# The merge-gate columns of a hybrid decoder trunk: from plain three-term matmuls to a seven-product Strassen form, with h parked in DRAM

## The chip, the cores and the metric

The kernel runs on one core of one Trainium2 chip, in one launch. The metric is the device time of one execution in microseconds (us); the kernel before takes 928.23 us (median of three runs, 928.15 to 928.38).

## The reference, cut to what matters

One layer of a decoder trunk with 1024 tokens and 1024 channels:

```
h = rms_norm(x, g_pre)
s5_x, s5_g, lru_x, lru_g, gate_s, gate_l = split(h @ w_in)   # 512, 512, 1280, 1280, 1024, 1024 columns
y_s = S5 branch of s5_x (complex diagonal state space), GELU, GLU, times silu(s5_g), @ w_bs
y_l = causal conv and RG-LRU of lru_x, times silu(lru_g), @ w_bl
merged = sigmoid(gate_s) * y_s + sigmoid(gate_l) * y_l
x = x + rms_norm(merged @ w_out, g_post)
x = x + (p @ w_ple) * sigmoid(x @ w_ple_gate)
```

The change concerns the last 2048 columns of `w_in`, those of `gate_s` and `gate_l`. In blocks of 128 columns they are the column blocks 28 to 35 and 36 to 43.

## The kernel before

Everything is laid out with channels on the partitions and tokens along the free axis. A matrix product is cut in blocks of 128 x 128 of the weight against 128 x 512 of the data (one half of the tokens). For accuracy each float32 operand is split in a rounded part and the rest (`hi`, `lo`), and one block product is three matmuls, in `three`: hi by hi, hi by lo of the data, lo of the weight by hi.

Weights come from DRAM in chunks of up to eight blocks into `wraw` (four buffers), and are split, four blocks (one *quad*) at a time, into a ring `wq` of six buffers. `weight_plan` lists the quads in order of use; `Weights.ahead`, called before each use, makes the quad four places ahead. `make` copies the quad with ScalarE to `hi`. The `lo` is a subtraction on VectorE (`lows`); for the late matrices named in `BY_DMA` it is made otherwise: ScalarE writes the negated hi, and a DMA of GpSimd's queue adds the raw weight onto it. Some matrices further on (w_bl, w_out) already are in a Strassen form, with sums of weights that `sum` makes on GpSimd.

`h` stands in four quarters, `hq["B11"]`, `"B12"`, `"B21"`, `"B22"` (half of the channels, half of the tokens), each with a hi and a lo page of 1 MB.

The instruction order on TensorE, VectorE, ScalarE and GpSimd is the order in which the code is written; only SyncE's DMAs are ordered by a scheduler. Work beside the matmuls is written as generators in a list `bg`, and `tick()` advances each by one step; the loops of matmuls call it at fixed places, so a step of the side work has its fixed place between two groups of matmuls on every engine. All engines work through their orders without overtaking.

The stage that is changed I call the *light stage*. In it `light(m, ...)` makes one column block: `rows` runs 48 matmuls (eight blocks of channels, two halves of tokens, three terms) with a tick after each 12, ScalarE takes the sigmoid, SyncE stores it (`sgl_d`, `sgs_d`). Eighteen columns come this way: 36 to 43, 28 to 35, and 4 and 5 (these with silu). The side work of this stage is the S5 branch, `s5_all`: eight blocks `hb` in `s5_main`, each a chain over all engines: TensorE `pkt` and `pin`, ScalarE `kt` and `pq`, VectorE `ta`, `tb`, four scans, `q`; eight small DMAs that spread `kt` into `toep`; GpSimd's `s5_out_weights` for the next block (it reuses the buffer of `kt`, tile `t`, and so waits until those DMAs have landed); then TensorE `py` from `toep` and `q`. After the light stage comes the LRU stage (`lru_head`), where the same ring of weights goes on.

Of the kernel before, what the change touches and what calls it, by code (L numbers as in the profile page):

```python
# [13 lines left out]
ALU = mybir.AluOpType  # L14
# [18 lines left out]

F_ROWS = (0, 1, 4, 2, 5, 3, 6, 7)


def weight_plan():
    blocks, quads = [], []

# [9 lines left out]
    def col(name, m, ks):  # L49
        return [(name, k, m) for k in ks]  # L50
# [21 lines left out]

    for m in range(NL):
        gated(8 + m, m - 1)
        plain(col("w_in", 18 + m, range(ND)))
# [32 lines left out]
    for h in range(2):  # L108
# [3 lines left out]
        for c in cs[0 if h else 2:]:  # L112
            cut(c)
    return blocks, quads


BLOCKS, QUADS = weight_plan()

# [17 lines left out]
class Weights:  # L136
# [42 lines left out]
    def sum(self, upto):  # L179
        G = self.nc.gpsimd  # L180
        while len(self.ready) <= min(upto, len(QUADS) - 1):
            i = len(self.ready)
            self.fetch(i)
            q = QUADS[i]
            s = self.sums
            if q[0] == "O2" and len(self.done) < i:
# [20 lines left out]
            if q[0] in ("S4", "O4"):  # L207
                add("S4", "A12", "S2", ALU.subtract, "S2")
            if q[0] == "S3":
# [3 lines left out]
    def make(self, upto):  # L213
        nc = self.nc
        while len(self.done) <= min(upto, len(QUADS) - 1):
# [7 lines left out]
            q = QUADS[i]  # L223
            if q[0] == "plain" and BLOCKS[q[1][0]][0] in self.BY_DMA and i < len(QUADS) - 2 * ND:
                nc.scalar.activation(lo, src, AF.Copy, scale=-1.0)  # L225
                nc.gpsimd.dma_start(lo.bitcast(F32), src, accum_op=ALU.add)  # L226
            else:
                self.owed.append((i, lo, src, hi))
# [24 lines left out]
def tile_hybrid_trunk(  # L253
# [19 lines left out]
    pages = ctx.enter_context(tc.tile_pool(name="pages", bufs=1))  # L273
    page_pool = {i: pages for i in range(14)}

# [9 lines left out]
    y_d = dram.tile([NS, 8, 8, 16, P], F32, name="y_d")  # L285
    pt_d = dram.tile([2, 8, 32 * P], F32, name="pt_d")

    def cst(shape, name, value=None, dt=F32):
# [617 lines left out]
    def s5_main(hb, table, before):  # L906
# [20 lines left out]
        for g in range(4):  # L927
            T.matmul(ps[32 * g:32 * g + 16, :P], bb_1[:, 4 * hb + g, :],
                     ca[:, g, 0:8, :].rearrange("p d c -> p (d c)"), start=True, stop=True, tile_position=(0, 32 * g))
        for g in range(4):  # L930
            S.activation(kt[:, g, :], ps[32 * g:32 * g + 16, :P], AF.Copy)
        V.tensor_tensor(kt[:, :, 0:16], kt[:, :, 0:16], dd, ALU.add)
        for j in range(8):
            nc.sync.dma_start(toep[j::8, :, 16 * j:P], kt[:, :, 0:P - 16 * j])
        yield

        pin = px.tile([P, 2, 2, P], F32, tag="px", name=f"pin{hb}")
        for g in range(4):
            T.matmul(pin[:, g // 2, g % 2, :], win[:, g, :], U[:, g, :], start=True, stop=True)
        next(table, None)  # L940
# [86 lines left out]
    def u_last():  # L1027
# [3 lines left out]
        yield  # L1031

    bg.append(u_last())
    bg.append(s5_all())
    for m in range(ND):
        light(36 + m, sgl_d[m], False, ev_tile)
    for m in range(ND):
        light(28 + m, sgs_d[m], False, ev_tile)
    for m in range(2):
        light(4 + m, sil_d[m], True, ev_tile)  # L1040
    drain()
    s5x.close()
# [85 lines left out]
    for m in range(NL):  # L1128
        conv, early, gate, gates = lru_head(m)
        conv(rows(hplain, f"rx{m}", between=between))  # L1130
        bg.append(early())
        gate(rows(hplain, f"rg{m}"))
        between = gates
# [564 lines left out]
```

## Time and profile before

| what | us |
|---|---|
| runs | 928.15, 928.23, 928.38 |
| profiled execution, own time | 928.25 |
| its span on the core | 926.5 |
| TensorE busy with matmuls | 919.0 |
| VectorE, ScalarE, GpSimd busy | 624.6, 469.1, 150.6 |
| light stage (first `ps_L` to first `ps_rx` matmul) | 78.0 to 300.6 |

PE is TensorE's matmuls, PEld its weight loads, DVE VectorE, ACT ScalarE, POOL GpSimd, SP SyncE's DMA queue. The profiled execution's own time is 1.75 us more than its span, and it stands at the median of the runs. A row of the trace names a line of the code, an engine, the tile written and read, and a duration; a matmul's own duration (0.39 us) overlaps its neighbours', so what a matmul costs is read from the distance of two starts.

### The profile page before, as it was taken

How to read it: one execution, taken by the hardware profiler on the slowest of the kernel's cores; microseconds unless marked ns; L12 is line 12 of the kernel's file. 1: busy time of each engine (PE TensorE's matmuls, PEld its weight loads, DVE VectorE, ACT ScalarE, POOL GpSimd, SP SyncE). 2: the span in 40 equal slices, each digit the busy share in tenths (PEclk: the TensorE clock that was granted, in tenths of full speed). 3: DMA queues.
4: the chain of work that ended last, by engine and by line, in shares of the span. 5: the costliest groups of instructions: out<-in, count | busy, mean ns of one | idle time of the engine just before them, and what ended most of it. 6: DMA issues, size and time to landing. Idle time of an engine off the chain costs nothing.

```text
span 926.5 us, 11716 instructions
## 1 busy us (share of the span) xinstructions
PE 919.0 (99%) x4228; PEld 760.3 (82%) x4228; DVE 624.6 (67%) x977; ACT 469.1 (51%) x714; POOL 150.6 (16%) x159
## 2 busy tenths in 40 slices
PE   9999999999999999999999999999999999999997
PEld 7888888888888888888888888888888887887886
DVE  6885566666664347766666767687862798886863
ACT  6643233444443356666666668544534355558531
POOL 1218112212220000000000000022322126422100
PEclk9999999999999999999999999999999999999999
DMA  9745445564533201111111116811479975499951
GB/s 358 277 126 160 126 142 166 172 171 133 173 97 113 74 29 52 52 46 51 52 52 52 47 34 216 291 56 55 141 255 244 247 193 206 119 245 233 301 184 56
DMA packets 70442, 134.21 MB, mean 145 GB/s; under 512 B 18416, under 2 KB 32880, under 8 KB 70384
## 3 DMA queue, kind: packets, MB, share of 16 engines
q1 hardware_dynamic: 64768, 122.72, 41.7%
q0 software_dynamic: 5472, 10.49, 6.3%
q8 instruction: 33, 0.54, 0.2%
q10 hardware_dynamic: 144, 0.26, 0.1%
q14 instruction: 25, 0.20, 0.1%
HBM read 95.30 MB, written 27.53 MB: 133 GB/s over the span
## 4 chain that ended last, share of the span: by engine, by line
PE 89%; issue 6%; DMA 2%; DVE 1%; POOL 1%; ACT 0%; POOLq 0%; SPq 0%
PE ps_L L319 16%; PE ps_L L317 8%; PE ps_rx L319 8%; PE ps_rg L319 8%; PE ps_rg L317 4%; PE ps_rx L317 4%; PE ps_F L319 3%; PE ps_u L319 3%; PE bZ L319 3%; PE ps_pg L319 2%; PE bW L319 2%; PE pg L319 2%; PE bX L319 2%; PE ps_ple L319 2%; PE ps_ea L319 2%
## 5 line engine op out<-in xcount | busy, mean ns | idle before, releaser
L319 PE MATMUL ps_L<-hB,wq 128*128 128x512 f32 x640 | 197.4, 390 | 0.0
L319 PEld LDWEIGHTS ps_L<-hB,wq 128*128 128x128 f32 x640 | 120.3, 188 | 24.3
L317 PE MATMUL ps_L<-hB,wq 128*128 128x512 f32 x320 | 127.1, 397 | 0.0
L222 ACT ACTIVATE wq<-wraw 128x512 fp32r<-128x512 f32 (+1 forms) x188 | 112.5, 613 | 24.1 <-issue 9.2
L234 DVE TENSOR_TENSOR wq<-wraw,wq 128x512 fp32r<-128x512 f32 (+1 forms) x152 | 105.0, 706 | 3.1 <-ACT wq L222 3.1
L319 PE MATMUL ps_rg<-hB,wq 128*128 128x512 f32 x320 | 98.5, 389 | 0.0
L319 PE MATMUL ps_rx<-hB,wq 128*128 128x512 f32 x320 | 98.5, 389 | 0.0
L319 PE MATMUL ps_pg<-x1hl,wq 128*128 128x512 f32 x240 | 74.9, 392 | 0.3 <-DVE x1hl L1374 0.2
L317 PEld LDWEIGHTS ps_L<-hB,wq 128*128 128x128 f32 x320 | 60.2, 188 | 13.3 <-issue 1.7
L319 PEld LDWEIGHTS ps_rg<-hB,wq 128*128 128x128 f32 x320 | 60.1, 188 | 12.5
L319 PEld LDWEIGHTS ps_rx<-hB,wq 128*128 128x128 f32 x320 | 60.1, 188 | 12.4
L194 POOL TENSOR_TENSOR wS<-wraw 128x512 f32<-128x512 f32 x8 | 12.4, 1549 | 354.8 <-DMA wraw<-w_blocks 343.3
L1078 DVE SCALAR_TENSOR_TENSOR c<-ps_rx,cp_t,c 128x1023 f32<-128x1023 f32 (+2 forms) x30 | 38.5, 1282 | 46.2 <-ACT c L1076 45.5
L317 PE MATMUL ps_rx<-hB,wq 128*128 128x512 f32 x160 | 62.3, 389 | 0.0
L317 PE MATMUL ps_rg<-hB,wq 128*128 128x512 f32 x160 | 62.3, 389 | 0.0
L319 PEld LDWEIGHTS ps_pg<-x1hl,wq 128*128 128x128 f32 x240 | 44.8, 188 | 11.5 <-DVE x1hl L1374 1.7
L1015 ACT ACTIVATE sg<-ps_L 128x1024 f32<-128x1024 f32 x20 | 20.5, 1027 | 59.7 <-issue 52.5
L226 POOL DMA_DIRECT2D wq<-wraw x36 | 31.8, 883 | 100.1 <-ACT wq L225 65.6
L317 PE MATMUL ps_pg<-x1hl,wq 128*128 128x512 f32 x120 | 47.0, 391 | 0.0
L319 PE MATMUL ps_u<-hB,wq 128*128 128x512 f32 x128 | 39.8, 392 | 0.4 <-DVE hB L736 0.4
L319 PE MATMUL ps_F<-ys,wq 128*128 128x512 f32 x128 | 39.4, 389 | 0.0
L1086 ACT ACT_TABLE_LOAD x9 | 11.5, 1283 | 51.2 <-DVE yr L1115 51.2
(360 smaller groups left out, 1927.0 us busy)
## 6 DMA issues: line engine op xcount, KB each, us to landing
wraw<-w_blocks SPq DMA_DIRECT2D x95, 512.0 KB
wq<-wraw POOLq DMA_DIRECT2D x36, 256.0 KB, 6.0
xt<-x_t SPq DMA_DIRECT2D x8, 512.0 KB
ple_d<-ple_sb SPq DMA_DIRECT2D x8, 512.0 KB
wn<-sbt SPq DMA_DIRECT2D x8, 512.0 KB
sgl_d<-sg SPq DMA_DIRECT2D x8, 512.0 KB
wn<-pt_d SPq DMA_DIRECT2D x16, 256.0 KB
sgs_d<-sg SPq DMA_DIRECT2D x8, 512.0 KB
```

Of the source, the lines that this page charges most:

```text
L194: G.tensor_tensor(s[name], s[a], s[b], op)
L222: nc.scalar.activation(hi, src, AF.Copy)
L226: nc.gpsimd.dma_start(lo.bitcast(F32), src, accum_op=ALU.add)
L234: self.nc.vector.tensor_tensor(lo, src, hi.bitcast(F32), ALU.subtract)
L317: T.matmul(ps, wh, xh, start=start, stop=False, skip_group_check=more)
L319: T.matmul(ps, a, b, start=False, stop=stop and a is (wh if xl_last else wl), skip_group_check=more)
L1015: S.activation(t, ps, AF.Sigmoid)
L1078: V.scalar_tensor_tensor(c[:, d:], ps[:, :NT - d], w_[3 - d], c[:, d:], ALU.mult, ALU.add)
L1086: S.activation(sq, ps, AF.Sigmoid)
```

## The change

Two neighbouring column blocks m and m+1 (the list `PAIRS` has the first of each) and two halves of the channels make a 2 x 2 matrix of weight quads A11, A12, A21, A22; `h` is the 2 x 2 matrix B11, B12, B21, B22. The eight products of quads become seven, by sums of both operands:

- Sums of weights, for each pair S1 = A21+A22, S2 = S1-A11, S3 = A11-A21, S4 = A12-S2, made on VectorE (the set `light` in `Weights.sum`), each used for one half of the tokens. `make` uses the DMA form of `lo` for all 56 of these quads.
- Sums of h, four quarters of them. `t_build` stages, for each of four channel blocks k, the hi of all four quarters (four DMAs of SyncE, `copies`), adds the lo (four adding DMAs of GpSimd's queue, `adds_`), then makes four differences on VectorE; ScalarE and VectorE split two of them (into the pages of `B12`, and pages 7 and 9), and two are stored to `tl_d` and later loaded and split by `t_last` into the pages of `B11` and `B21`, when these are not needed any more.
- The plain h is stored to `h_d` first (`h_pages_out`, six DMAs of 1 MB) and loaded back at the end (`h_back`).
- The order is by operand. Columns 4 and 5 come first. Then a stage that I call *X*: 16 products, B11 and B21 by the plain quads A11 and A12 of each pair's first column block (names `lX`, `lx`); half of the sums goes to `lu_d`. Then a stage *Z*: for each of the eight pairs five products (names `lZ`, `lc`), with sums in PSUM on VectorE. One product (`lprod`) is 12 matmuls, one quad, one tick. I call that a *slot*.
- `s5_main` loses one step: `pin` is issued with `pkt`.
- The LRU stage's first column block pair (8 and 18) takes its quads in another order, so that B22 is used first and B21 last; one chunk of weights is loaded a second time for it.
- GpSimd's descriptor space is halved to make room for page 19.

On GpSimd's queue where the S5 blocks begin, before (`ca`, `t9`, `dd` are S5's; nothing else stands between them):

```order
L896 TENSOR_TENSOR cc_705<-cc_705,sgn_128 128x512
L902 TENSOR_TENSOR ca0_1085<-pw_134,cc_705 128x576
L903 TENSOR_TENSOR t9_0_1086<-pw_134,cc_705 128x576
L904 TENSOR_TENSOR ca0_1085<-ca0_1085,t9_0_1086 128x576
L917 TENSOR_TENSOR dd0_1094<-ident_89,d_skip_130 16x64
L902 TENSOR_TENSOR ca1_1200<-pw_134,cc_705 128x576
L903 TENSOR_TENSOR t9_1_1201<-pw_134,cc_705 128x576
L904 TENSOR_TENSOR ca1_1200<-ca1_1200,t9_1_1201 128x576
```

and after, in stage X (`wq` rows are the adding DMAs for the weights' lo, `lt` rows those of `t_build`):

```order
L241 DMA wq25_1177<-wraw14_866 128x512
L1074 DMA lt2_1164<-hB111_377 128x512
L1074 DMA lt2_1164<-hB121_379 128x512
L1074 DMA lt2_1164<-hB211_445 128x512
L1074 DMA lt2_1164<-hB221_447 128x512
L241 DMA wq26_1209<-wraw15_962 128x512
L241 DMA wq27_1266<-wraw15_962 128x512
L920 TENSOR_TENSOR ca1_1296<-pw_137,cc_708 128x576
L921 TENSOR_TENSOR t9_1_1297<-pw_137,cc_708 128x576
L922 TENSOR_TENSOR ca1_1296<-ca1_1296,t9_1_1297 128x576
L1074 DMA lt3_1253<-hB111_377 128x512
L1074 DMA lt3_1253<-hB121_379 128x512
```

The lo of the weights, the adding DMAs for h and S5's products now stand in one line on one engine.

On ScalarE at the same place, before (`wq` rows make a quad's hi, `sg` is the sigmoid of a column, `kt` and `pq` are S5's):

```order
L1015 ACTIVATE sg_38_1063<-ps_L38_985 128x1024
L222 ACTIVATE wq22_1067<-wraw13_824 128x512
L222 ACTIVATE wq23_1114<-wraw13_824 128x512
L931 ACTIVATE kt0_1129<-pkt0_1130 16x128 x4
L1015 ACTIVATE sg_39_1169<-ps_L39_1066 128x1024
L222 ACTIVATE wq24_1173<-wraw14_900 128x512
L946 ACTIVATE pq0_1190<-pin0_1160 64x256 x4
L222 ACTIVATE wq25_1225<-wraw14_900 128x512
```

and after (two `wq` rows for a quad, hi and negated hi; `hB120` and `lt1_7` are the hi copies of `t_build`'s differences, `lx` those of a product's result):

```order
L236 ACTIVATE wq24_1136<-wraw14_866 128x512
L240 ACTIVATE wq24_1136<-wraw14_866 128x512
L1088 ACTIVATE hB120_378<-lt1_1090 128x512
L1089 ACTIVATE lt1_7_1088<-lt1_1090 128x512
L1130 ACTIVATE lx2_1134<-lX2_1133 128x512
L236 ACTIVATE wq25_1177<-wraw14_866 128x512
L240 ACTIVATE wq25_1177<-wraw14_866 128x512
L1130 ACTIVATE lx3_1135<-lX2_1133 128x512
L236 ACTIVATE wq26_1209<-wraw15_962 128x512
L240 ACTIVATE wq26_1209<-wraw15_962 128x512
```

Quad 25 now is made behind the two copies that need `t_build`'s differences of k = 1.

On VectorE, one S5 block from `ta` to `q`, before:

```order
L950 TENSOR_TENSOR ta3_1642<-pq3_1757,tt3_1548 128x512
L951 TENSOR_TENSOR tb3_1643<-pq3_1757,tt3_1548 128x512
L952 TENSOR_TENSOR q3_1762<-ta3_1642,tb3_1643 128x256
L953 TENSOR_TENSOR q3_1762<-ta3_1642,tb3_1643 128x256
L234 TENSOR_TENSOR wq34_1719<-wraw19_1396,wq34_1719 128x512
L960 SCALAR_TENSOR_TENSOR q3_1762<-r8_131,q3_1762 128x128 x4
```

and after, in stage Z (`lZ` rows are the sums in PSUM, L208 the sums of weights):

```order
L966 TENSOR_TENSOR ta4_2053<-pq4_2172,tt4_1934 128x512
L967 TENSOR_TENSOR tb4_2054<-pq4_2172,tt4_1934 128x512
L968 TENSOR_TENSOR q4_2177<-ta4_2053,tb4_2054 128x256
L969 TENSOR_TENSOR q4_2177<-ta4_2053,tb4_2054 128x256
L1150 TENSOR_TENSOR lZ3_2147<-lZ3_2147,lc3_2034 128x512
L208 TENSOR_TENSOR wraw27_1980<-wraw26_1978,wraw27_1980 128x512
L976 SCALAR_TENSOR_TENSOR q4_2177<-r8_134,q4_2177 128x128 x4
L886 TENSOR_TENSOR tt5_2141<-etab_894 128x2x128
L886 TENSOR_TENSOR sb5_2142<-etab_894 128x2x128
L980 TENSOR_TENSOR ta4_2053<-q4_2177,tt4_1934 128x512
L981 TENSOR_TENSOR tb4_2054<-q4_2177,tt4_1934 128x512
L1156 TENSOR_TENSOR lZ3_2147<-lZ3_2147,lc3_2034 128x512
```

With one more L208 before the last four `q` rows, four operations of the light stage's own stand inside this chain where one stood before.

The diff, cut to its core:

```diff
+PAIRS = (36, 38, 40, 42, 28, 30, 32, 34)
...
-    for m in (*range(36, 44), *range(28, 36), 4, 5):
+    for m in (4, 5):
         plain(col("w_in", m, range(ND)))
+    for i in range(0, len(PAIRS), 2):
+        for ks in (lo, hi):
+            c = chunk([b for m in PAIRS[i:i + 2] for b in col("w_in", m, ks)])
+            light.add(c)
+            cut(c)
+    for m in PAIRS:
+        c0, c1 = (chunk(col("w_in", m + i, range(ND))) for i in range(2))
+        light.add(c0)
+        quads.extend((part, c0, c1, 4) for part in ("O2", "S1", "S3", "S4", "A22"))
...
+    head = [chunk(col("w_in", 8, ks) + col("w_in", 18, ks)) for ks in (hi, lo)]
+    for c in (*head, head[0]):
+        cut(c)
...
-                G.tensor_tensor(s[name], s[a], s[b], op)
+                (self.nc.vector if light else G).tensor_tensor(s[name], s[a], s[b], op)
...
-            if q[0] == "plain" and BLOCKS[q[1][0]][0] in self.BY_DMA and i < len(QUADS) - 2 * ND:
+            if q[1] in LIGHT or (q[0] == "plain" and BLOCKS[q[1][0]][0] in self.BY_DMA
+                                 and i < len(QUADS) - 2 * ND):
                 nc.scalar.activation(lo, src, AF.Copy, scale=-1.0)
                 nc.gpsimd.dma_start(lo.bitcast(F32), src, accum_op=ALU.add)
...
-        yield
-
-        pin = px.tile([P, 2, 2, P], F32, tag="px", name=f"pin{hb}")
-        for g in range(4):
-            T.matmul(pin[:, g // 2, g % 2, :], win[:, g, :], U[:, g, :], start=True, stop=True)
         next(table, None)
         yield
...
+    def t_build():
...
+        def copies(k):
+            if k < 4:
+                stage[k] = quarter(page((19, 8)[k % 2], f"lt{k}", F32))
+                for j, n in enumerate(("B11", "B12", "B21", "B22")):
+                    nc.sync.dma_start(stage[k][:, j], hq[n][0][:, k, :].bitcast(F32))
+        def adds_(k):
+            if k < 4:
+                for j, n in enumerate(("B11", "B12", "B21", "B22")):
+                    G.dma_start(stage[k][:, j], hq[n][1][:, k, :].bitcast(F32), accum_op=ALU.add)
+        copies(0)
+        yield
+        adds_(0)
+        yield
...
+        for k in range(4):
+            s11, s12, s21, s22 = (stage[k][:, j] for j in range(4))
+            copies(k + 1)
+            V.tensor_tensor(s11, s12, s11, ALU.subtract)
+            V.tensor_tensor(s12, s22, s12, ALU.subtract)
+            V.tensor_tensor(s22, s22, s11, ALU.subtract)
+            V.tensor_tensor(s21, s21, s22, ALU.subtract)
+            S.activation(hq["B12"][0][:, k, :], s22, AF.Copy)
+            S.activation(lt1[0][:, k, :], s11, AF.Copy)
+            yield
+            adds_(k + 1)
...
+            nc.sync.dma_start(tl_d[0, k], s12)
+            nc.sync.dma_start(tl_d[1, k], s21)
+            yield
...
+    def lprod(ps, op, start):
+        W.ahead()
+        for k, wb in enumerate(W.next()):
+            three(ps, wb, (op[0][:, k, :], op[1][:, k, :]), start and k == 0, k == 3, not start)
+        tick()
...
     bg.append(u_last())
+    bg.append(h_pages_out())
     bg.append(s5_all())
-    for m in range(ND):
-        light(36 + m, sgl_d[m], False, ev_tile)
-    for m in range(ND):
-        light(28 + m, sgs_d[m], False, ev_tile)
     for m in range(2):
         light(4 + m, sil_d[m], True, ev_tile)
+    bg.append(t_build())
+    for a in range(0, len(PAIRS), 2):
...
+            lprod(x_[:, HALF[i]], hq["B11"], True)
+            S.activation(cs[i][:, HALF[0]], x_[:, HALF[i]], AF.Copy)
+            nc.sync.dma_start(lu_d[a + i], cs[i][:, HALF[0]])
...
+            lprod(x_[:, HALF[i]], hq["B21"], False)
+            gate_out(PAIRS[a + i], 0, cs[i][:, HALF[1]], x_[:, HALF[i]])
...
+        lprod(z, hq["B12"], True)
+        V.tensor_tensor(z, z, u, ALU.add)
+        S.activation(u, z, AF.Copy)
+        lprod(w_, lt1, True)
+        S.activation(gb, w_, AF.Copy)
+        V.tensor_tensor(w_, w_, u, ALU.add)
+        lprod(z, hq["B11"], False)
+        V.tensor_tensor(gb, gb, z, ALU.add)
+        gate_out(m + 1, 1, gb, gb)
+        lprod(w_, hq["B22"], False)
+        gate_out(m, 1, u, w_)
+        lprod(z, hq["B21"], False)
+        gate_out(m + 1, 0, o21[:, p_ % 4], z)
...
-    nc = bacc.Bacc("TRN2", target_bir_lowering=False, num_devices=1)
+    nc = bacc.Bacc("TRN2", target_bir_lowering=False, num_devices=1, dynamic_dma_scratch_size=8192)
```

More of the change, by code (lines that the diff above doesn't have):

```diff
@@ L113, in weight_plan @@
             cut(c)
-    return blocks, quads
-BLOCKS, QUADS = weight_plan()
+    return blocks, quads, light
+BLOCKS, QUADS, LIGHT = weight_plan()
 FIRST = ("O2",)
@@ L1129, in tile_hybrid_trunk @@
         conv, early, gate, gates = lru_head(m)
-        conv(rows(hplain, f"rx{m}", between=between))
-        bg.append(early())
-        gate(rows(hplain, f"rg{m}"))
+        if m == 0:
+            ps = [wide(f"ps_r{n}0") for n in "xg"]
+            for t, q, hs in ((0, 1, (1,)), (1, 1, (1,)), (0, 0, (1, 0)), (1, 0, (1, 0)), (0, 1, (0,)), (1, 1, (0,))):
+                W.ahead()
+                wb = W.next()
+                for h in hs:
+                    for k in range(4):
+                        three(ps[t][:, HALF[h]], wb[k], hplain(4 * q + k, h), k == 0 and q == h, k == 3 and q != h)
+                if t == 1 and hs == (0,):
+                    break
+                tick()
+                if hs == (0,):
+                    conv(ps[0])
+            bg.append(early())
+            tick()
+            gate(ps[1])
+        else:
+            conv(rows(hplain, f"rx{m}", between=between))
+            bg.append(early())
+            gate(rows(hplain, f"rg{m}"))
         between = gates
```

68 lines of the change are left out of this document (64 added, 4 removed).

## The prediction

> **What bounds the kernel now.** I read the page first, then the waits of TensorE, then the light stage by windows, then the single engines in it.
>
> ```profile
> span 926.5 us, 11716 instructions
> PE 919.0 (99%) x4228; PEld 760.3 (82%) x4228; DVE 624.6 (67%) x977; ACT 469.1 (51%) x714; POOL 150.6 (16%) x159
> ```
>
> TensorE is busy for 99% of the span. The waits of TensorE by what they waited for (us in total, times, longest):
>
> ```profile
> PE warm L500 <- DVE halfpi L291: 1.1, 1, 1.1
> ...
> PE ps_pg L319 <- DVE x1hl L1374: 0.2, 1, 0.2
> ```
>
> Five waits, none above 1.1 us. So a matmul taken away is time taken away, as long as nothing new makes TensorE wait. What a matmul costs is the distance between starts:
>
> ```profile
> L317 PE MATMUL ps_L<-hB,wq x320: 388/389/500, 78.0 to 566.4; 128*128 128x512 f32 x160
> L317 PE MATMUL ps_rx<-hB,wq x160: 388/389/390, 300.6 to 529.7; 128*128 128x512 f32 x160
> 111.11 0.39 PE L317 MATMUL ps_L<-hB,wq 128*128 128x512 f32 x1
> 111.79 0.39 PE L317 MATMUL ps_L<-hB,wq 128*128 128x512 f32 x1
> 78.00:300.60 222.60, 222.60 (x1126) 184.56 (x1125) 139.19 (x270) 83.95 (x143) 50.27 (x54) 1.00 0.49 144
> 0.00:23.20 23.20, 21.35 (x83) 17.48 (x84) 15.05 (x18) 15.35 (x19) 4.15 (x10) 1.00 0.93 358
> 810.00:870.00 60.00, 59.76 (x277) 48.96 (x276) 47.00 (x87) 40.96 (x71) 16.33 (x19) 1.00 0.97 255
> ```
>
> Three matmuls start every 0.68 us, 0.2268 us each. The first two rows bound the light stage: 78.0 to 300.6. The last three are windows: length, then busy us of PE, PEld, DVE, ACT, POOL, then granted clock, DMA share, GB/s. In the light stage the clock is 1.00 and TensorE never idle, VectorE works 139 of 222.6 us, ScalarE 84, GpSimd 50, and the DMA engines move 144 GB/s. The other two windows are the busiest for DMA: 358 GB/s when the inputs are loaded, and 255 GB/s at a share of 0.97 late in the kernel, where many of the weights' lo come by adding DMAs.
>
> **The change part by part.** *Matmuls.* Before, 16 columns of 48; after, 56 quads of 12. That is 768 - 672 = 96 fewer: 96 x 0.2268 = **-21.8 us**. The S5 matmuls stay. The stage then has 200.8 us of matmuls.
>
> *Elementwise work.* The rows that price it, in the light stage (mean ns before the bar's end):
>
> ```profile
> L234 DVE TENSOR_TENSOR wq<-wraw,wq 128x512 fp32r<-128x512 f32 x31 | 22.2, 715 | 0.0
> L222 ACT ACTIVATE wq<-wraw 128x512 fp32r<-128x512 f32 x32 | 19.3, 622 | 0.1
> L946 ACT ACTIVATE pq<-pin 64x256 f32<-64x256 f32 x32 | 12.1, 377 | 6.0 <-issue 5.7
> L931 ACT ACTIVATE kt<-pkt 16x128 f32<-16x128 f32 x32 | 8.6, 268 | 13.7 <-issue 10.9 <-PE pkt L928 2.6
> L1015 ACT ACTIVATE sg<-ps_L 128x1024 f32<-128x1024 f32 x16 | 16.4, 1027 | 53.7 <-issue 46.6 <-PE ps_L L319 7.1
> ```
>
> VectorE loses 32 lo subtractions and gains 32 sums of weights of the same size (nothing net), 24 sums in PSUM and 32 operations for the sums of h, 56 x 0.7 = +39 us: 178 of 200.8. ScalarE goes from 32 to 112 operations on weights (+50 us), has 32 sigmoids of 512 for 16 of 1024 (+3.5) and 40 copies more (+25): 84 + 78 = 162 of 200.8. By sums alone both still fit under the matmuls. So neither adds time as a total; what counts is who stands behind whom.
>
> *Stage X: the sums of h in the queues of the weights.* The lo of all 56 quads now comes by GpSimd's adding DMA, and so does half of `t_build`'s sum. Such DMAs stand in the trace late in the kernel (duration of the issue, and time to landing, min/median/max):
>
> ```profile
> L226 POOL DMA_DIRECT2D wq<-wraw x36: 850/859/1209, 698.5 to 867.5; - x36
> DMA to landing us min/median/max: 3.2/6.0/11.1
> ```
>
> Call the landing time L. The differences of block k on VectorE wait for the last of four adding DMAs. ScalarE's two copies wait for the third difference, and the next quad's hi stands behind them; GpSimd's DMA for its lo stands behind that, and the four adding DMAs of k+1 behind this. From the second difference of k to that of k+1: two differences 1.4, two copies and one eviction 1.9, hi and negated hi 1.2, one lo issue 0.86, three more issues 2.6, then L: 7.9 + L. TensorE's pace would be two slots. The first round: stage X begins at 99.8 (78.0 + 96 x 0.2268); one slot 2.7, a copy 0.6, a quad 1.2, five issues to the last adding DMA's start 3.4: 107.7, landing at 107.7 + L. Three rounds and, after the last, 1.4 + 1.9 + 1.2 + L to the lo of the quad for slot 14: 135.9 + 5L. Without waits slot 14 would need it at 99.8 + 0.35 + 13 x 2.72 + 3.27 (S5) + 0.45 = 139.2. TensorE is late by 5L - 3.3: 12.7 us at L = 3.2, 26.7 at 6.0, 52.2 at 11.1. I take L = 7, **+31.7 us**: near the median, above it because this stage asks for more. By the listing it moves about 31 MB (the `lt`, `tl`, `lu`, gate and weight transfers, S5's loads) in 51 us, 600 GB/s, where the busiest rows have 358 and 255.
>
> The trace's shortest landing for such a DMA is 3.2 us and the median 6.0. The Trainium skill, "DMA: Bandwidth & Descriptors", section on the anatomy of one DMA by GpSimd's path, gives about 2.0 us plus bytes at 436 GB/s, which is 2.6 us for 256 KB; by it the delay here would be an estimated 9.7 us instead of 31.7. The row is of a queue with other traffic beside it, as here, so the row decides.
>
> *Stage Z: the S5 loop in fewer slots.* One S5 block had seven ticks, and has six:
>
> ```profile
> 141.68 0.41 PE L928 MATMUL pkt<-ca,bb 128*16 128x128 f32 x8
> 144.88 1.05 PE L939 MATMUL pin<-U,wn 128*128 128x128 f32 x8
> 159.39 0.38 PE L983 MATMUL py<-U,toep 128*128 128x128 f32 x2
> 161.09 0.48 PE L317 MATMUL ps_L<-hB,wq 128*128 128x512 f32 x1
> 164.00 0.41 PE L928 MATMUL pkt<-ca,bb 128*16 128x128 f32 x8
> 150.13 1.33 POOL L903 TENSOR_TENSOR t<-pw,cc 128x576 f32<-128x576 f32 x1 [9.80 <-DMA toep<-kt]
> 151.54 1.43 POOL L904 TENSOR_TENSOR ca<-ca,t 128x576 f32<-128x576 f32 x1
> 192.28 0.69 DVE L950 TENSOR_TENSOR ta<-pq,tt 128x512 f32<-128x512 f32 x1 [2.75 <-ACT pq L946]
> 201.81 0.42 DVE L972 TENSOR_TENSOR q<-ta,tb 64x254 f32<-64x254 f32 x1
> ```
>
> The cycle is 164.00 - 141.68 = 22.32 us, of which 84 matmuls are 19.05 and S5 3.27. With 72 matmuls it would be 19.6 us. Two chains must fit in it. (a) `pkt` to `pkt` over VectorE: after `pkt` (0.35), `kt` copies 1.1, an eviction 0.6, a quad 1.2 and `pq` 1.5, `ta` starts at 4.8; to the end of `q` it was 201.81 + 0.42 - 192.28 = 9.95, now with three more operations 12.05; `py` 161.09 - 159.39 = 1.7; a slot 2.72: 21.3 us. (b) over GpSimd: from `pkt` to `t` 150.13 - 141.68 = 8.45, the two products 2.8, then the lo DMA that now stands behind them, L, and the rest of its slot 2.3: 13.5 + L = 20.5 at L = 7. The longer decides: 21.3 - 19.6 = 1.7 us for each of seven cycles, **+11.9 us**. Ends: nothing, if the evictions fall in gaps; and at L = 11.1 chain (b) is 24.6, +35 us.
>
> *The turn to the LRU stage.* B12 and B11 (4.2 MB) are asked for after the first and third of the last pair's five products and are needed some 19 us later; at 255 GB/s they take 16.5. B21 has 16 us for 2.1 MB. SyncE's six issues of them stand ahead of two weight chunks, which the ring covers for four slots. I cost this at nothing, covered by the B22 products that now come first; if that cover fails it is up to 5 us. The six stores of `h_pages_out` wait for nobody late; but they delay `t_build`'s first copies, which is inside the range of L. The halved descriptor space and the second load of one chunk: nothing, under the same cover.
>
> *Sum.* -21.8 + 31.7 + 11.9 = +21.8 on the span: 926.5 + 21.8 = 948.3. The profiled execution took 1.75 us more than its span (928.25 against 926.5) and stands at the median of the runs (928.23): **950 us**.
>
> **The rivals.** *The landings are short* (ends on the other side). In stage X, if the adding DMAs land as fast as the trace's shortest, 3.2 us, TensorE is late by 12.7 only; with the S5 chains inside their cycle that gives 926.5 - 21.8 + 12.7 + 1.75 = 919. It decides at 5L - 3.3 = 21.8, L = 5.0 us, or lower as Z costs something. For it: nothing else used this queue before in that stage, and its DMA share is 0.49. Against: the median is 6.0 and the bytes rise. By the Trainium skill's figure, given above, this would be the likely case.
>
> *The whole build is hidden*: `t_build` has its stage buffers ready so early that the ring's four slots cover every round; then the gain is whole, 906 us. Against it: 7.9 + L for each round against 6.5 us for two slots, in order on three engines.
>
> *The DMA engines become the bound.* The queue rows of the page (packets, MB, share of 16 engines):
>
> ```profile
> q1 hardware_dynamic: 64768, 122.72, 41.7%
> q0 software_dynamic: 5472, 10.49, 6.3%
> ```
>
> SyncE's queue takes 0.417 x 926.5 / 122.72 = 3.15 us of all engines per MB, GpSimd's adding one 5.6. The light stage had 0.49 x 222.6 = 109 us. Added are 29.9 MB on the first (h out and back 12.6, stage copies 4.2, `tl` 4.2, `lu` 4.2, nine chunks of weights 4.7) and 72 x 0.262 = 18.9 MB on the second: 94 + 105 us. Without h's way back, 20 us of which falls in the next stage, that is 288 us, at a share of 0.97 297 against 222.6 before: 928 + 75 = 1003. For it: the sum. Against: the window of 358 GB/s has a share of 0.93, 2.6 us per MB, so the price per MB falls where transfers are long.
>
> **How the numbers follow.** A difference of 0.2% (1.9 us) is about what a measurement of this kernel tells from none. The forecast, with its own range 930 to 985 (L from 5 to 9, Z from 0 to 20 us), has 0.62; short landings 0.15; all hidden 0.09; DMA bound 0.14. The range 911 to 990 leaves out the hidden case and most of the DMA-bound one, about 0.2. Faster: 0.15 + 0.09 = 0.24; the same 0.03, where L is just at 5; slower 0.73.
>
> **What would show it.** Right: matmuls into `lX` and `lZ` count 672, starts 0.227 us apart in a group; TensorE has waits in stage X on the adding DMAs into `wq`, some 30 us, and VectorE waits there on those into `lt`; the rounds of `t_build` are about 15 us apart; in Z `pkt` comes every 21 to 22 us; no wait at the first `ps_rx`. Wrong: rounds of 8 us, a landing below 5 us, a Z cycle of 19.6; or DMA shares near 1 all through with landings over 10.

## The result, and the profile after

The changed kernel takes 1069.9 us (median of four runs, 1063.2 to 1072.6) against 928.2 us before in the same session: 1.152 times the time, 95% interval 1.146 to 1.157. The forecast was 950 us with a range of 911 to 990. It had the right sign and far too small a size.

The head of the page after:

```profile
span 1061.4 us, 12103 instructions
PE 938.4 (88%) x4132; PEld 760.4 (72%) x4132; DVE 659.8 (62%) x1035; ACT 536.4 (51%) x852; POOL 209.7 (20%) x231
```

TensorE has 96 matmuls fewer and is busy 19.4 us longer. It is idle for 1061.4 - 938.4 = 123.0 us, against 926.5 - 919.0 = 7.5 before. Taking the 96 matmuls at the prediction's 0.2268 us, it should be busy for 919.0 - 21.8 = 897.2. So the span's 134.9 us more are 115.5 of idle time and 41.2 of slower matmuls, less 21.8.

All but 1.3 us of it lies in the light stage. Windows of stage X, of stage Z, and of the whole (length; busy us of PE, PEld, DVE, ACT, POOL; granted clock, DMA share, GB/s), and the first matmuls of the LRU stage:

```profile
99.00:214.00 115.00, 64.73 (x246) 48.36 (x245) 46.37 (x83) 41.52 (x80) 37.22 (x41) 0.76 0.96 262
214.00:434.00 220.00, 156.88 (x689) 120.33 (x689) 116.04 (x203) 102.22 (x189) 60.51 (x61) 0.88 0.70 182
78.00:434.00 356.00, 242.60 (x1027) 186.07 (x1026) 174.55 (x328) 150.80 (x279) 109.41 (x125) 0.85 0.78 207
L335 PE MATMUL ps_rx<-hB,wq x160: 389/389/395, 434.2 to 663.5; 128*128 128x512 f32 x160
```

The light stage takes 434.2 - 78.0 = 356.2 us where it took 222.6; what follows takes 627.2 where it took 625.9. In X no engine is busy for more than 65 of 115 us, in Z none but TensorE for more than 117 of 220. So the engines wait for each other, or, in X, for the DMA engines with their share of 0.96. What TensorE waited for there (us in total, times, longest):

```profile
PE lX L335 <- ACT lx L1130: 38.6, 8, 14.9
PE lZ L335 <- ACT lc L1151: 29.5, 8, 7.3
PE lZ L335 <- DVE lZ L1156: 14.1, 8, 3.1
PE lZ L335 <- ACT lc L1116: 12.9, 8, 3.9
PE lX L335 <- ACT lx L1116: 11.7, 4, 5.3
PE lZ L335 <- DVE lc L1160: 6.6, 6, 1.8
```

These are 113.4 us, all but two of the 115.5. None of these rows is on an adding DMA into `wq`, which the prediction had put in this place. Each is a first matmul of a product (L335) that waits until ScalarE or VectorE has *read a result out of PSUM*. Why these evictions are late is seen on ScalarE in X (start, duration, instruction, idle time before it and what ended it):

```profile
132.39 0.62 ACT L240 ACTIVATE wq<-wraw 128x512 fp32r<-128x512 f32 x1
143.18 0.63 ACT L1088 ACTIVATE hB<-lt 128x512 fp32r<-128x512 f32 x1 [10.17 <-DVE lt L1086]
143.72 0.61 ACT L1089 ACTIVATE lt<-lt 128x512 fp32r<-128x512 f32 x1
144.24 0.58 ACT L1130 ACTIVATE lx<-lX 128x512 f32<-128x512 f32 x1
```

ScalarE stands idle for 10.2 us in front of `t_build`'s copy L1088, which waits for VectorE's difference L1086. VectorE had itself waited just before, at the end for a DMA into `lt`:

```profile
141.73 0.69 DVE L1085 TENSOR_TENSOR lt<-lt 128x512 f32<-128x512 f32 x1 [1.76 <-DMA lt<-hB]
```

The eviction L1130 stands behind the copy, and TensorE waits for the eviction. Four of X's twelve waits are of this kind, 36.0 of the 50.3 us. Two at the start of X, 8.9 us, have another reason:

```profile
116.25 0.60 ACT L1130 ACTIVATE lx<-lX 128x512 f32<-128x512 f32 x1 [8.01 <-DMA sil_d<-sg]
```

Here the eviction itself must wait: it writes one of two buffers (`ev_tile`), and the store of what stood in it (`sil_d`, of the columns before) has not ended. The other six waits are of 0.7 to 1.5 us.

And once TensorE has waited for some time, it is slower for a while. Rows of TensorE in Z, where one group of three should take 0.68 us:

```profile
274.29 0.80 PE L335 MATMUL lZ<-hB,wq 128*128 128x512 f32 x1 [2.45 <-ACT lc L1116]
274.88 1.06 PE L337 MATMUL lZ<-hB,wq 128*128 128x512 f32 x2
275.73 0.63 PE L335 MATMUL lZ<-hB,wq 128*128 128x512 f32 x1
277.01 0.63 PE L335 MATMUL lZ<-hB,wq 128*128 128x512 f32 x1
```

From 275.73 to 277.01 a group takes 1.28 us. The granted clock of 0.76 in X and 0.88 in Z, against 1.00 in this stage before, says the same.

### The profile page after: what moved, and what is told of

Same layout as the page of the kernel before. It is cut to its first block, busy times and chain, and to the rows that moved or that the text cites. A ratio compares the mean times of both kernels' runs of the same rounds, so it can differ in the third digit from the quotient of the medians.

```text
span 1061.4 us, 12103 instructions
## 1 busy us (share of the span) xinstructions
PE 938.4 (88%) x4132; PEld 760.4 (72%) x4132; DVE 659.8 (62%) x1035; ACT 536.4 (51%) x852; POOL 209.7 (20%) x231
## 4 chain that ended last, share of the span: by engine, by line
PE 53%; DVE 3%; issue 3%; ACT 1%; DMA 1%; POOL 1%; POOLq 0%; ACTq 0%; DVEq 0%
PE ps_rx L337 7%; PE ps_rg L337 7%; PE ps_rx L335 3%; PE ps_rg L335 3%; PE ps_pg L337 3%; PE bZ L337 2%; PE ps_F L337 2%; PE pg L337 2%; PE bW L337 2%; PE bX L337 2%; PE ps_pg L335 2%; PE ps_ea L337 1%; PE ps_eb L337 1%; PE ps_L L337 1%; PE bZ L335 1%
## 5 line engine op out<-in xcount | busy, mean ns | idle before, releaser
L236 ACT ACTIVATE wq<-wraw 128x512 fp32r<-128x512 f32 (+1 forms) x198 | 119.2, 613 | 31.9 <-issue 10.4
L241 POOL DMA_DIRECT2D wq<-wraw x76 | 68.2, 917 | 238.2 <-ACT wq L240 178.1
L249 DVE TENSOR_TENSOR wq<-wraw,wq 128x512 fp32r<-128x512 f32 (+1 forms) x122 | 83.9, 705 | 14.2 <-ACT wq L236 14.1
L335 PE MATMUL lZ<-hB,wq 128*128 128x512 f32 x128 | 55.9, 436 | 33.6 <-DVE lZ L1156 14.1
L337 PE MATMUL lZ<-hB,wq 128*128 128x512 f32 x256 | 83.9, 411 | 0.0
L208 POOL TENSOR_TENSOR wS<-wraw 128x512 f32<-128x512 f32 x8 | 12.0, 1497 | 341.7 <-DMA wraw<-w_blocks 330.2
L335 PE MATMUL lX<-hB,wq 128*128 128x512 f32 x64 | 31.7, 496 | 50.3 <-ACT lx L1130 38.6
L335 PE MATMUL ps_rx<-hB,wq 128*128 128x512 f32 x160 | 62.2, 389 | 0.0
L335 PE MATMUL ps_rg<-hB,wq 128*128 128x512 f32 x160 | 62.2, 389 | 0.0
L337 PEld LDWEIGHTS lZ<-hB,wq 128*128 128x128 f32 x256 | 51.6, 202 | 10.6
L335 PEld LDWEIGHTS lZ<-hB,wq 128*128 128x128 f32 x128 | 25.7, 200 | 46.4 <-DVE lZ L1156 17.1
L335 PEld LDWEIGHTS lX<-hB,wq 128*128 128x128 f32 x64 | 14.9, 233 | 58.6 <-ACT lx L1130 42.5
L337 PE MATMUL lX<-hB,wq 128*128 128x512 f32 x128 | 48.0, 463 | 0.0
L240 ACT ACTIVATE wq<-wraw 128x512 fp32r<-128x512 f32 x76 | 47.0, 619 | 0.0
L335 PE MATMUL ps_pg<-x1hl,wq 128*128 128x512 f32 x120 | 46.9, 391 | 0.0
```

The lines of the kernel that those rows point to most:

```text
L208: (self.nc.vector if light else G).tensor_tensor(s[name], s[a], s[b], op)
L236: nc.scalar.activation(hi, src, AF.Copy)
L249: self.nc.vector.tensor_tensor(lo, src, hi.bitcast(F32), ALU.subtract)
L335: T.matmul(ps, wh, xh, start=start, stop=False, skip_group_check=more)
L337: T.matmul(ps, a, b, start=False, stop=stop and a is (wh if xl_last else wl), skip_group_check=more)
```

## The experiments

Two theories stood at the start. *Evictions*: TensorE waits for reads of PSUM, for two reasons. The two running sums of a pair are the halves of one PSUM tile of two banks (`wide`), and a matmul into one half waits for the readers of the other; and the readers stand in queues behind blocked instructions. *Load*: the DMA engines in X (share 0.96) and S5's chain in Z are what everything waits for, and the names of the waits are incidental. Line numbers differ between the versions; the names of tiles do not.

**Idle time alone, in the kernel before.** Does the clock fall because TensorE waits?

```diff
-        S.activation(t, ps, AF.Sigmoid)
+        for _ in range(7):
+            S.activation(t, ps, AF.Sigmoid)
...
+    pw2 = gap_ctx.enter_context(tc.tile_pool(name="pw1", bufs=1, space=PSUM))
```

> The kernel before, with one PSUM tile for all columns of the light stage and each column's sigmoid done seven times: TensorE gets a gap of about 7.3 us after each of 18 columns, with no new DMA traffic. Theory (gaps lower the granted clock): clock 0.75 to 0.9 in the light stage, matmuls there longer than 0.39 us after a gap, the stage 380 us or more, the time over 1085 us. Rival (the clock fell for the DMA load or the power of other engines): clock 1.00, the stage 354 us, the time 1060 us.

Measured, in one execution: 1127.7 us. The largest wait of TensorE and the window from 78 us to 500:

```profile
PE ps_L L317 <- ACT sg L1016: 127.8, 16, 10.0
78.00:500.00 422.00, 274.81 (x1178) 219.76 (x1179) 134.46 (x273) 198.97 (x256) 44.57 (x53) 0.82 0.25 79
```

The clock is 0.82 with a DMA share of 0.25, and TensorE's busy time over the whole span is 960.3 us for the same matmuls that took 919.0. So waiting alone lowers the clock and costs 41.3 us on top of itself; neither DMA traffic nor the new operations are needed for it.

**The same with short gaps** (`range(1)` in place of `range(7)`).

> The kernel before with one PSUM tile for all columns of the light stage and each sigmoid done once, so gaps of about 1.2 us after each column of 10.9 us. Theory (any gap lowers the granted clock for a while after it): clock about 0.9 in the light stage, and the stage longer than its 20 us of waits by another 8 us or more: over 955 us. Rival (only gaps of several us lower the clock): clock 1.00 and a time of 945 to 950 us, the waits alone.

Measured, in one execution: 985.9 us, busy 937.4. Two gaps with the matmul after them, and windows behind gaps of 4.35 and of 3.6 us and over a stretch with gaps of 1.2 us only:

```profile
178.99 0.79 PE L317 MATMUL ps_L<-hB,wq 128*128 128x512 f32 x1 [4.35 <-ACT sg L1016]
338.63 0.50 PE L317 MATMUL ps_L<-hB,wq 128*128 128x512 f32 x1 [2.42 <-DVE sg L1018]
180.00:184.00 4.00, 4.00 (x11) 2.90 (x9) 0.00 (x0) 0.00 (x0) 0.00 (x0) 0.55 0.37 145
211.00:215.00 4.00, 3.10 (x7) 2.48 (x8) 0.08 (x1) 1.36 (x2) 0.00 (x0) 0.50 0.15 34
225.00:240.00 15.00, 13.84 (x75) 11.01 (x74) 6.74 (x15) 5.03 (x9) 1.23 (x1) 1.00 0.30 101
```

My sentence "any gap lowers the clock" is wrong, and so is the rival's "only the waits count". Behind the long gaps the clock is about half for some 4 us; gaps of 1.2 us leave it at 1.00, and the window from 338 to 342 us, behind the one of 2.42, has 1.00 too. The time came out above 955 us because several gaps were longer than meant, up to 4.4 us.

**Sums in PSUM tiles of their own.** In X and Z six tiles of one bank take the place of three of two.

```diff
-        x_ = wide(f"lX{a}")
+        x_ = [half_bank(f"lX{a + i}") for i in range(2)]
...
-        z, w_ = (v[:, HALF[i]] for v in (wide(f"lZ{p_}"),) for i in range(2))
+        z, w_ = (half_bank(f"l{c}{p_}") for c in "ZW")
```

> The change, with the two running sums of a pair in PSUM tiles of their own (six tiles of one bank in stages X and Z in place of three of two banks), nothing else. Theory: the 113 us of TensorE waits in X and Z are waits for the eviction of the other half of the same tile, and the low granted clock follows from them. Then the waits on lx and lc evictions shrink to under 40 us, the clock in both stages returns to 0.95 or more, and the time is 920 to 965 us; what is left in X is waits on the adding DMAs into wq, as the prediction had it. Rival (the DMA engines are full in X, and the S5 chain is too long in Z): other waits of the same length take their place, and the time stays above 1040 us.

Measured: 1024.3 us, 1.103 times before (1.100 to 1.106); 45.6 us less than the change, and short of what I expected. The waits:

```profile
PE lX L335 <- ACT lx L1137: 53.3, 4, 25.9
PE lZ L335 <- ACT lc L1158: 28.1, 6, 7.6
```

and ScalarE in X:

```profile
145.28 0.63 ACT L1088 ACTIVATE hB<-lt 128x512 fp32r<-128x512 f32 x1 [15.26 <-DVE lt L1086]
146.33 0.58 ACT L1137 ACTIVATE lx<-lX 128x512 f32<-128x512 f32 x1
```

Z lost about half of its waits, X none, and X's clock is 0.73, not the 0.95 of the expectation. Even with a tile of its own a running sum must be read before the next product is added onto it, one slot later, and in X the read stands behind `t_build`'s copy (two of the four waits, 44.0 of the 53.3 us).

**Without the adding DMAs of `t_build`,** with the shared tiles, and with the tiles apart:

```diff
         def adds_(k):
-            if k < 4:
+            if k < 0:
```

> The change with t_build's sixteen adding DMAs left out (so the sums of h lack the lo of h), two banks to a tile as in the change. Theory: the X waits are ScalarE's evictions standing behind the copies of t_build, which wait for the adding DMAs; without these the rounds of t_build fall from 18.8 to about 10 us, the X waits from 50 to about 20 us, Z keeps its 63 us: 1025 to 1045 us. Rival (X's waits are of the tile alone, whoever stands in ScalarE's queue): X keeps its 50 us, and the time stays at 1060 or more.

> Tiles of their own for the two sums of a pair and t_build's sixteen adding DMAs left out, both. Theory: nothing is left in X that makes TensorE wait over 5 us in all, Z has at most the 11.9 us of the S5 chain: 905 to 925 us, faster than before. Rival (S5's chain or the DMA engines bound Z): Z is over 165 us long and the time above 935 us.

Measured: 1051.9 us (1.135, 1.132 to 1.139) and 1009.1 us (1.087, 1.085 to 1.089). Both are worse than expected, and in the second the rival's signs came: Z takes 182 us, over its 165, and the time is over 935. The adding DMAs are worth 18.0 us of the change and 15.3 of the version with the tiles apart, not the whole of X's waits. The rounds of `t_build` in the version with shared tiles:

```profile
L1085 DVE TENSOR_TENSOR lt<-lt x4: 692/692/693, 103.9 to 161.9; 128x512 f32<-128x512 f32 x4
```

(161.9 - 103.9) / 3 = 19.3 us for a round, as long as with them (18.8). So a round is as long without the adding DMAs, and L alone does not explain its length. Nor do the staging copies: in this run's X VectorE never waits for a DMA into `lt`. ScalarE waits for 11.0 us in front of `t_build`'s copies and for 22.8 us in front of evictions, for stores (`sil_d`, `lu_d`, `sgs_d`) that still hold the buffer. Left are the queues themselves and the DMA traffic; the next run takes out both kinds of staging DMA.

**The sums straight from the pages of h,** on VectorE, with no staging DMAs at all; tiles apart.

```diff
-                    nc.sync.dma_start(stage[k][:, j], hq[n][0][:, k, :].bitcast(F32))
...
+            V.tensor_tensor(s22, hi["B22"], lo["B22"], ALU.add)
+            V.tensor_tensor(s12, hi["B12"], lo["B12"], ALU.add)
+            V.tensor_tensor(s11, s12, hi["B11"], ALU.subtract)
+            V.tensor_tensor(s11, s11, lo["B11"], ALU.subtract)
+            V.tensor_tensor(s12, s22, s12, ALU.subtract)
+            V.tensor_tensor(s22, s22, s11, ALU.subtract)
...
```

> Tiles of their own for the two sums of a pair, and the sums of h made by VectorE straight from the pages of h (40 operations in place of 16), so that t_build has no staging copies and no adding DMAs (33.6 MB less of DMA writes and reads together). Theory (ScalarE's evictions stood behind t_build's two copies, which stood behind VectorE, which waited for DMAs): the 53 us of waits on lx evictions fall under 10 us, stage X takes 55 to 65 us in place of 112, its clock is over 0.93, Z keeps its 28 us of waits: 950 to 970 us. Rival (VectorE, or the DMA traffic of weights and S5, is what X waits for): X stays over 85 us and the time over 985 us.

Measured: 993.9 us (1.070, 1.068 to 1.072), 30.4 us less than with the tiles apart alone. The waits:

```profile
PE lZ L335 <- ACT lc L1149: 27.9, 6, 7.6
PE lX L335 <- ACT lx L1128: 21.0, 5, 7.0
```

X's fell from 53 to 21, Z's stayed. Part of the step is as expected; 21 us is more than the 10 I had allowed, X takes 82 us, between the two expectations, and the time is the rival's. Half of the 21 us (two waits, 10.5) still stands behind the copy, for which VectorE now has six operations in a row to do, behind other work of its own. The other half (three waits, 10.5) stands behind evictions that wait for a store.

**The same in one tile**, to see whether the two causes act apart.

> The change with the direct sums by VectorE alone, the two running sums of a pair in one PSUM tile of two banks as in the change. Theory (both causes act apart: the block in ScalarE's queue, and the tile shared by two sums): 1030 to 1045 us, some 43 us more than with direct sums and tiles apart, with over 50 us of waits in Z. Rival (sharing the tile costs only while the queue is blocked): under 1010 us.

Measured: 1039.7 us (1.120, 1.117 to 1.123), 45.8 us above the run before it; the tiles were worth 45.6 with the staging DMAs and 42.9 without the adding ones. The shared tile has a price of its own, whatever blocks ScalarE's queue.

**S5 held back until after Z,** first with the tiles apart, then with the shared tile. Only stages X and Z are comparable; S5 then runs alone.

```diff
+        while not held:
+            yield
         for hb in range(8):
             before = yield from s5_main(hb, s5_table(hb + 1) if hb < 7 else iter(()), before)
...
+    held.append(1)
     drain()
```

> As the run with direct sums, but the eight blocks of S5 held back until after stage Z, where TensorE has nothing else: the whole time is not comparable (S5 alone adds over 100 us), only stages X and Z are. Theory (Z's evictions are late because they stand behind S5's instructions on VectorE and ScalarE): no waits on lc over 3 us in all, Z's 480 matmuls in 109 to 113 us at clock 1.00. Rival (the chain product, sum on VectorE, copy on ScalarE is itself longer than the one slot of 2.7 us between): Z keeps 20 us or more of waits.

> As the run with direct sums in one tile (two sums in a tile of two banks), with S5's eight blocks held back until after stage Z; only stages X and Z are comparable. Theory (the shared tile has a price of its own: each product waits until VectorE and ScalarE have read the other half, with nothing else in their queues some 0.7 to 2 us for each of four products a pair): 25 to 45 us of waits in Z, Z 135 to 160 us long against 111 with tiles apart. Rival (the shared tile costs only where S5 makes the evictions late): under 8 us of waits, Z under 120 us.

One execution each. Stage Z with the tiles apart, and all of TensorE's waits in it; then stage Z with the shared tile, and its waits:

```profile
171.00:282.00 111.00, 110.10 (x480) 88.99 (x478) 40.38 (x63) 64.88 (x121) 32.41 (x39) 1.00 0.98 248
PE lW L335 <- DVE lW L1158: 0.5, 1, 0.5
PE lZ L335 <- ACT lc L1153: 0.4, 2, 0.2
```

```profile
171.00:327.00 156.00, 120.07 (x485) 88.65 (x488) 40.78 (x62) 65.76 (x120) 32.28 (x38) 0.99 0.76 191
PE lZ L335 <- ACT lc L1146: 12.1, 8, 2.1
PE lZ L335 <- DVE lZ L1151: 11.4, 8, 1.4
PE lZ L335 <- ACT lc L1111: 6.3, 8, 1.0
PE lZ L335 <- DVE lc L1155: 6.2, 8, 0.8
```

This pair says most. With tiles of their own and nothing else in the queues, Z's 480 matmuls take 111 us: 0.23 us each, clock 1.00, no waits to speak of. The DMA engines are then at a share of 0.98, so a full share alone makes TensorE wait for nothing here, and for Z the DMA half of the load theory falls. Sharing the tile makes the stage 45 us longer, 36.0 of it in waits, four in each pair, none over 2.1 us, at a clock of 0.99; the rest shows as TensorE's busy time, 120.1 us for 110.1. S5 is the rest: with S5 in its place the version with tiles apart has 33 us of waits in Z and a stage of about 180 us. This pair does not tell S5's own length from evictions that stand behind its operations, but the trace of the run with direct sums shows the second. In front of its wait of 7.25 us, to 222.54, VectorE works without a gap from 209.41 on an S5 block and two sums of weights, and the sum that the eviction needs starts at 221.17 behind them.

In X of the version with tiles apart 17.1 us of waits are left without any S5, at a DMA share of 0.97. Of these 13.2, in four of five waits, stand behind evictions that wait for a store, as here, where the wait of TensorE is 6.4 us:

```profile
162.63 0.60 ACT L1132 ACTIVATE lx<-lX 128x512 f32<-128x512 f32 x1 [9.52 <-DMA sgs_d<-lx]
```

So for X the load theory holds in part: stores that end late keep the buffers of the evictions.

**Five tiles a pair.** If waiting for a running sum is the trouble, no product should be added onto an earlier one: each of Z's five products in a tile of its own, summed by VectorE.

```diff
-        lprod(z, hq["B11"], False)
-        V.tensor_tensor(gb, gb, z, ALU.add)
+        lprod(z1, hq["B11"], True)
+        V.tensor_tensor(o, z1, u, ALU.add)
+        V.tensor_tensor(z1, z1, gb, ALU.add)
...
```

> As the run with direct sums, and in Z each of a pair's five products in a PSUM tile of its own, summed by VectorE out of PSUM (six operations a pair in place of three, two copies by ScalarE fewer), so that no product waits for the eviction of an earlier one of its pair; S5 as in the change. Theory: the waits on lc are gone, Z has under 10 us of waits and a clock over 0.95: 912 to 930 us. Rival (VectorE, with 24 operations more, becomes the bound of Z): Z over 150 us, time over 945 us.

Measured: 988.3 us (1.065, 1.063 to 1.067); the rival was nearer. Z takes 173 us, over its 150, though VectorE is busy for only 127 of them, so its total is not the bound. The waits on `lc` are gone but for one of 4.1 us at the first `ps_rx`, and others came:

```profile
PE py L1000 <- DVE q L988: 10.0, 5, 4.1
PE lW L337 <- DMA wq<-wS: 6.7, 1, 6.7
```

Now S5's own chain is late: `py` waits for VectorE's `q`, and the weights' lo is late in one place.

**`t_build`'s copies one slot later,** on top of the five tiles, so that ScalarE need not wait for VectorE.

```diff
             V.tensor_tensor(s22, s22, s11, ALU.subtract)
+            yield
             S.activation(hq["B12"][0][:, k, :], s22, AF.Copy)
```

> As the run with five tiles, but t_build's two copies on ScalarE are issued one slot after the sums that they read, and the lo two slots after, with the sums of the next k; the sums for B21 are made by GpSimd at the end of the build. Theory (what is left in X is evictions behind copies that wait for VectorE): the 23 us of waits on lx fall under 8 us, X takes under 68 us in place of 82, and the time is 955 to 970 us. Rival (VectorE itself is too full in X, 19.7 of 20 us in one window): X stays over 78 us, time over 980 us.

Measured: 982.2 us (1.058, 1.056 to 1.060), the best version found, and still slower than before. X takes 74 us, between the two expectations, and the time is the rival's. Some of its largest waits:

```profile
PE lX L335 <- ACT lx L1135: 17.4, 4, 10.3
PE py L1000 <- DVE q L988: 6.5, 6, 3.1
PE lA L337 <- DMA wq<-wraw: 6.0, 2, 4.2
```

Of the 17.4 us 10.3 is one wait behind a copy, the other 7.1 stand behind stores. With `lW`, `lB` and `lC` the waits on the weights' lo are 18.0 us; this is the kind of wait that the prediction had named, but in Z and not in X. TensorE is busy for 919.4 of 981.6 us: 62.2 idle, and 22.2 more than the 897.2 of full clock.

**The sums of weights on GpSimd,** on top of that, to relieve VectorE in Z.

```diff
-                (self.nc.vector if light else G).tensor_tensor(s[name], s[a], s[b], op)
+                G.tensor_tensor(s[name], s[a], s[b], op)
```

> As the run with the copies a tick later, and the sums of the weights of these columns made by GpSimd, as for the other quads, in place of VectorE: VectorE loses 24 operations of 0.7 us in Z. Theory (S5's chain over VectorE sets the S5 cycle of 28.8 us in Z): the cycle falls under 27 us, and the time by 5 to 15 us against the run with the copies a tick later. Rival (GpSimd's queue, where the sums now stand with the lo DMAs and S5's products, becomes the wait): waits on wq grow, and the time is the same or longer.

Measured: 1006.4 us (1.084, 1.081 to 1.087), 24.3 us *more* (32 operations went over, not the 24 that I named). The time is the rival's, the reason neither's: the waits on `wq` fell, but `py` waits for `q` for 37.0 us in place of 6.5, the S5 cycle grew from 28.5 us to 31.1, and VectorE's instructions themselves became slow. TensorE's wait with the change, then VectorE's `q` between 170 and 340 us without the change (first) and with it (second; mean ns of one ahead of the last bar):

```profile
PE py L1000 <- DVE q L988: 37.0, 9, 8.8
L987 DVE TENSOR_TENSOR q<-ta,tb 64x254 f32<-64x254 f32 x14 | 9.0, 642 | 0.2
L987 DVE TENSOR_TENSOR q<-ta,tb 64x254 f32<-64x254 f32 x12 | 14.0, 1168 | 0.2
```

The same instruction takes 642 ns in the mean in one and 1168 in the other, and VectorE, with 32 instructions fewer, is busy for 707.6 us instead of 690.1. The single rows say when: with the change a `q` row takes 0.42 us where GpSimd has no elementwise work (four rows from 277.76) and 4.30 where two of its sums of weights run beside it (243.28). Without the change the three slow rows of L987 (1.41 to 1.60 us) also have an operation of GpSimd's beside them.

## Why the prediction was wrong where it was

*Matmuls, -21.8 us:* right. `lX` and `lZ` have 192 and 480 records of matmuls, and where nothing disturbs them 480 take 110.1 us.

*Elementwise totals "cost nothing; what counts is who stands behind whom":* right as a total. Forecast were 178 us for VectorE and 162 for ScalarE; they work 174.6 and 150.8 in the stage.

*Stage X, +31.7 us:* the step that failed is "two copies and one eviction 1.9". The eviction entered the sum as time of ScalarE and not as something that TensorE waits for. The chain was followed to the lo of a quad only, which the ring covers for four slots; the eviction behind the same copies has one slot, and in a shared tile none. So the waits came at once, 50.3 us of them, six of the twelve 4.2 to 14.9 us long. Of these, 8.9 us came from a term that the sum did not have at all, stores that still held the buffer of an eviction. The inputs were not far off: in X the adding DMAs landed after 9.3 us in the median into `lt` and 7.0 into `wq` for L = 7, and the rounds took 18.8 us for 14.9. By the prediction's own sum, 9.3 in its four landings into `lt` and 7.0 in its last into `wq` would make 40.9 us in place of 31.7 (an estimate). That the size is near is in part luck: without the adding DMAs, on whose L I had hung the range, the time fell by only 15 to 18 us, and the rounds were as long.

```profile
lt<-hB POOLq DMA_DIRECT2D x16, 256.0 KB, 9.3
wq<-wraw POOLq DMA_DIRECT2D x12, 256.0 KB, 7.0
L1085 DVE TENSOR_TENSOR lt<-lt x4: 691/693/693, 123.5 to 179.9; 128x512 f32<-128x512 f32 x4
L946 PE MATMUL pkt<-ca,bb x64: 272/278/283, 154.1 to 403.1; 128*16 128x128 f32 x64
```

*Stage Z, +11.9 us:* the same step in another place. The cycle was reckoned as S5's chains against 72 matmuls that only run, 21.3 us. It is (403.1 - 154.1) / 7 = 35.6 us, the last row above, and still (402.93 - 237.46) / 5 = 33.1 for the cycles that lie in Z alone. What failed is the silent premise that products follow each other at 0.2268 us. Each pair has four places where a product waits for a read of PSUM, and those reads stand among S5's instructions, which in turn wait for TensorE. The sum has nothing for the two halves of a tile either; they lie in different banks, but the waits go by tile, which is worth 45.6 us of the whole. The order of TensorE's own instructions, with what each waits for, has this in it; the prediction mostly followed the orders of the other three engines.

*The clock:* every matmul was costed at the clock of 1.00 of the stage before. That was a property of a stage without gaps. The 41.2 us are a term that the sum did not have. The Trainium skill, "TensorE: Matmul & The Clock Gate", section "Why this matters for your kernels", says that TensorE idle for more than about 3 us falls back to half its clock. The long gaps agree: half behind 3.6 and 4.35 us. So do short ones: 0.99 over a stage with 32 waits of up to 2.1. In between the runs show no sharp limit. In the change the clock is 0.50 behind a wait of 2.87 us (390.36) and 1.00 behind one of 2.53 (285.44), both behind long matmuls; behind S5's short `pkt` and `pin` it is 0.50 to 0.51 after waits of 2.45, 2.67 and even 1.77 us (274.29, 342.67, 372.61). And the same wait of 2.42 us in front of X's first product, behind long matmuls, is followed by a clock of 0.50 in the first version with the tiles apart and of 1.00 in the one with the weights' sums on GpSimd (windows behind it, columns as above):

```profile
102.90:106.00 3.10, 3.10 (x9) 2.42 (x8) 0.82 (x3) 0.00 (x0) 0.41 (x1) 0.50 0.98 303
102.90:106.00 3.10, 3.10 (x17) 2.53 (x17) 3.00 (x6) 0.56 (x2) 0.00 (x0) 1.00 1.07 398
```

So the length of the last wait alone does not decide; what else does is not shown.

*The turn to the LRU stage, nothing:* right; no wait at the first `ps_rx` in the change.

*The rivals:* the DMA engines' sum was good, 288 us forecast and 0.78 x 356 = 278 measured, but the stage grew past it for other reasons, and in Z a share of 0.98 went with no waits. In X they did count: with S5 held back and no staging DMAs 13.2 us of waits stand behind stores that ended late, at a share of 0.97. Whether the bandwidth or the order of SyncE's queue makes those stores late, no run separates. The rival of short landings falls with the 9.3 and 7.0 us.

*What would have shown it:* the count of matmuls and VectorE's waits on `lt` came true. The waits on `wq` in X did not, nor did a `pkt` every 21 to 22 us, and those false places are the sign that the mechanism was wrong, not only its size.

What stays open is whether any order makes it a gain. The best version is 54 us away, with waits left on the weights' lo (18.0 us), on X's evictions (17.4) and on S5's chain (6.5), and 22 us of slower matmuls.

## What to carry to other kernels

When a change adds a read of PSUM between two products onto the same sum, cost that read as a wait of TensorE with one product's time of slack, and ask who stands ahead of it in ScalarE's and VectorE's queues, and which store still holds the buffer that it writes; two sums that alternate want tiles of their own. When the forecast has waits of several microseconds on TensorE, add the slower clock behind them: here 41 us on 116. Moving work off a busy queue helps only if the engine that takes it does not slow the first one down.

## What the runs showed of the hardware that I had not expected

Idle time has a second price, which depends on how it is cut: 158 us of added idle time, mostly in gaps of about 8 us, cost 41.3 us of slower matmuls, while 36.0 us in waits of at most 2.1 left the clock at 0.99. Between them one and the same wait of 2.42 us halved the clock in one version and not in another.

GpSimd's elementwise work slows VectorE's: 642 to 1168 ns in the mean for the same instruction, and 0.42 to 4.30 us for single rows of it without and with GpSimd's sums beside them. The Trainium skill, "SBUF — State Buffer", section "Who interferes with whom", says that VectorE and GpSimd share a pair of ports to SBUF under an exclusive lock. The lengthening is what such a lock would give; no run here shows the lock itself.
